# One matmul of 512 moving columns, high and low parts of h side by side, in place of two of 256 with the same weights

## The chip, the cores and the metric

The kernel runs on 1 core of one Trainium2 chip. The time is the device time of one execution in microseconds (us), taken as the median of the runs shown. TensorE multiplies: a block of 128x128 weights is loaded (the stationary operand) and the moving columns stream past it into PSUM, a memory of eight banks, each with 512 fp32 values per partition. VectorE (DVE) and ScalarE (ACT) read PSUM and work in SBUF, GpSimd (POOL) does a few large passes, SyncE (SP) issues nearly all DMAs.

## The reference

One decoder layer, batch 1, 256 tokens (S), 2048 channels (D), fp32:

```
h = LN(x)
p = h @ w_in                 # 3 groups: RG-LRU, block-sparse attention (NSA), attention into mem
h = LN(alpha*h + concat(lru, nsa, mem) @ w_out)
h = LN(alpha*h + (gelu(g) * u) @ w_down)     # g, u = causal conv3(h @ w_up)
```

`w_in` has 3608 columns, `w_up` 11264 (two times 5632), `w_out` and `w_down` 2048. The results are wanted in fp32.

## The kernel before

All large products run in fp32r, a format in which TensorE takes a 128-row by N-column moving operand in one pass but keeps fewer bits than fp32. To get the bits back each operand is split into a high part (its value rounded to fp32r) and a low part (what is left). A product a·b is then formed as aH·bH + aL·bH + aH·bL, three matmuls into one PSUM group.

**The weight stream.** The weights come as a list of chunks (`steps`) of 128 x 1024 fp32, 512 KB each. `advance` keeps four raw loads in flight (SP), has ACT write the high part (`wH`, line 127) and DVE the low part (`wL`, line 135) two to three chunks before the products use them. `run` takes chunk by chunk: `advance`, the chunk's products (`mm`), what follows them (`after`), and a round of background work (`pump`). Each engine works through its instructions in the order in which the code wrote them, and starts one when those it depends on are done; nothing else orders the work.

**Stages, in order.** Keys and values of mem (lines 272 and 205 to 208), the input norm that fills the tiles of h, the input projection in blocks of 128 channels, with the attention heads and the LRU as background work, the output projection (0.31 to 0.40 ms of the trace), the first norm, the up projection (0.41 to 0.90 ms), the down projection and the last norm.

**Channel-major blocks.** The input projection's 28 blocks and the up projection's 88 are computed by `t_mm`: one block of 128 channels is two chunks of eight 128x128 weight blocks. Per weight block of `wH` there is a matmul with the high part of h (`hH`, line 194) and one with the low part (`hL`, line 195), both of 256 moving columns (the tokens); then eight matmuls of `wL` with `hH` (line 197). So a chunk is 24 matmuls, a block 48, and the sum stands in 256 columns of a bank (`acc`, three banks, or `sc`, two). h lies in eight tiles `h0` to `h7` of four channel blocks each, the first four for high parts, the last four for low parts.

**Reading the bank.** For the up projection, `after` lets ACT write scale times bank plus bias (line 870), two DVE operations add the shifted taps from the bank (line 873), ACT applies gelu to the first half of a pair (line 876), DVE multiplies the second half in (line 878), and ACT and DVE split the product into `actH` and `actL` (lines 187, 188). In the input projection ACT or DVE copies the bank out (lines 375, 397, 429, 497), or ACT and DVE form a convolution from it (387, 390), or DVE adds an embedding to it (421).

**Token-major blocks.** Output and down projection (`proj`, `m_mm`, lines 205 to 208) use the activations as weights and the chunk as moving operand, 512 columns a matmul. In their last column block some chunks are held in other tiles (`alt`): in the down projection in `h0` to `h7`, where h is no longer needed.

Of the kernel before, what the change touches and what calls it, by code (L numbers as in the profile page):

```python
# [41 lines left out]
# column offsets in the per-partition parameter array  # L42
# [9 lines left out]
NP1 = _P["convw"].start          # up to here: parameters kept for the whole kernel  # L52
# [3 lines left out]
def hymba_layer(ctx, tc, x, memT, params, rows, wab, w1, wmem, win, wvg, wout, wup, wdn, out):  # L56
# [13 lines left out]
    hq = [fix.tile([128, 4, S], F32R, name="h%d" % i) for i in range(8)]  # L70

    def hH(kt, cols=slice(0, S)):
        return hq[kt // 4][:, kt % 4, cols]

    def hL(kt, cols=slice(0, S)):
        return hq[4 + kt // 4][:, kt % 4, cols]
# [11 lines left out]
    # ---------------------------------------------------------------- weight stream  # L88
# [26 lines left out]
    def part_tile(j, k, name, bufs):  # L115
        if steps[j]["alt"]:
            pool, names = steps[j]["alt"]
            return pool().tile([128, NE], F32R, name=names[k])
        return ws.tile([128, NE], F32R, name=name, bufs=bufs)
# [23 lines left out]
    def advance():  # L143
        """the loads run ahead of the high parts, those one chunk ahead of the low parts, those LOOK chunks ahead
        of the products"""
# [10 lines left out]
    def pump(rounds):  # L156
        """one stage of every live chain a round; at most one chain starts in a round"""
# [27 lines left out]
    # ---------------------------------------------------------------- helpers  # L185
# [4 lines left out]
    def t_mm(acc, h, l, kts, first, last):  # L190
        n = len(kts)
        for a, kt in enumerate(kts):
            w = h[:, a * 128:(a + 1) * 128]
            T.matmul(acc, w, hH(kt), start=(first and a == 0), stop=False, skip_group_check=True)  # L194
            T.matmul(acc, w, hL(kt), start=False, stop=False, skip_group_check=True)  # L195
        for a, kt in enumerate(kts):
            T.matmul(acc, l[:, a * 128:(a + 1) * 128], hH(kt), start=False,  # L197
                     stop=(last and a == n - 1), skip_group_check=True)

# [21 lines left out]
    # ---------------------------------------------------------------- first loads  # L221
# [23 lines left out]
    # loads that follow those of a chunk of the weight stream  # L245
# [6 lines left out]
    # ---------------------------------------------------------------- memory keys and values  # L252
# [46 lines left out]
    # ---------------------------------------------------------------- input norm  # L299
# [19 lines left out]
    def to_hT(tp, kt0, nk, cols, g, b, eng):  # L319
        """tp: psum [128, nk, n], channels on partitions; gain and bias, then both parts into the tiles of h"""  # L320
# [9 lines left out]
        split_act(hq[kt0 // 4][:, k:k + nk, cols], hq[4 + kt0 // 4][:, k:k + nk, cols], tv)  # L330

    def transposed(m, kt0, nk, tag):
        """normed rows of half m, channel blocks kt0.., channels on partitions"""
# [20 lines left out]
    # ---------------------------------------------------------------- input projection, channel-major blocks  # L354
    def win_blocks(cols, done, interleave=False):
        cur = {}

        def half(a, col, hf):
            def mm(h, l):
                if hf == 0:  # L360
                    cur[a] = pp.tile([128, S], F32, name="acc", bufs=3)
# [9 lines left out]
    # memory queries  # L371
    def done_qmem(a, bank):
        if a == 0:
            qms[0] = mx.tile([128, 4, S], F32, name="qmem")
        A.activation(qms[0][:, a, :], bank, AF.Copy)
        bg.append(mem_attention(a))

    # LRU input: causal convolution straight from PSUM
    xc = {}

    def done_lrux(a, bank):
# [3 lines left out]
        src = bank  # L385
        cw = lambda k: P("convw", a * 4 + k)
        A.activation(t, src, AF.Identity, scale=cw(3), bias=P("convb", a))
# [6 lines left out]
    def done_q(a, bank):  # L394
        if a == 0:
            qns[0] = mx.tile([128, 4, S], F32, name="qn")
        A.activation(qns[0][:, a, :], bank, AF.Copy)
# [13 lines left out]
    def done_cmp(a, bank):  # L411
        """stack token parities on partitions and add the position embedding"""
        src = bank.rearrange("p (n l two) -> p n l two", l=8, two=2)
# [14 lines left out]
    def done_kk(a, bank):  # L428
        A.activation(kk[:, a, :], bank, AF.Copy)
# [27 lines left out]
    # block compression  # L457
# [33 lines left out]
    # LRU output gate  # L491
    ygs = {}

    def done_lruy(a, bank):
        if a % 4 == 0:
            ygs[a // 4] = mx.tile([128, 4, S], F32, name=("qmem", "kmem")[a // 4])
        V.tensor_copy(ygs[a // 4][:, a % 4, :], bank)
# [568 lines left out]
```

## Time and profile before

| | |
|---|---|
| median of 3 runs | 1156.81 us (1154.85 to 1161.25) |
| profiled execution, span from first to last instruction | 1158.0 us |
| PE busy | 1125.6 us, 97% |
| DVE busy | 739.9 us, 64% |
| ACT busy | 568.3 us, 49% |
| matmuls, lines 194, 195 and 197 | 1856 each (1152 into `acc`, 704 into `sc`) |

The profile is one execution. Matmuls overlap in it, so that a busy PE says only that it never stood still. What one matmul costs in a row of them is the distance from start to start: the length of a stretch divided by the number of matmuls that started in it. A row of the view by stretches counts also the one or two that were still running when the stretch began.

### The profile page before, as it was taken

The page shows a single profiled execution, that of the slowest core. Times are in us where ns is not written, and L with a number is a line of the kernel's source. Part 1 is how long each engine was busy: PE and PEld are TensorE (multiplying, and loading weights), DVE is VectorE, ACT ScalarE, POOL GpSimd, SP SyncE. Part 2 cuts the span into 40 slices and gives each one's busy share as a digit, 9 for nine tenths or more (in the row PEclk, how much of TensorE's full clock was granted, in tenths as well). Part 3 has the DMA queues.
Part 4 walks back from the last instruction along what each step waited for, and adds up shares of the span by engine and source line. Part 5 has one row for each costly group of instructions (what it writes and reads, how often), then busy time and mean ns, then how long its engine had stood idle before and what let it go on. Part 6 is the DMA issues. An engine that isn't in the chain of part 4 may idle for free.

```text
span 1158.0 us, 19330 instructions
## 1 busy us (share of the span) xinstructions
PE 1125.6 (97%) x7848; PEld 1033.7 (89%) x7848; DVE 739.9 (64%) x1063; ACT 568.3 (49%) x832; POOL 44.7 (4%) x39
## 2 busy tenths in 40 slices
PE   8979999999999899999999999999999999999995
PEld 7879877899988799999999999999999888888884
DVE  6895555566765776666666666666666845454556
ACT  5635445456743465555555545555555433434340
POOL 0360000000000010000000000000000000000002
PEclk9989999999999999999999999999999999999998
DMA  9646432244566565555656556565565776666661
GB/s 340 235 171 194 148 109 90 91 141 134 182 200 191 172 209 191 184 186 181 202 186 193 185 180 200 179 204 182 183 190 178 231 244 193 191 192 193 190 195 77
DMA packets 58984, 211.81 MB, mean 183 GB/s; under 512 B 6544, under 2 KB 6672, under 8 KB 58768
## 3 DMA queue, kind: packets, MB, share of 16 engines
q1 hardware_dynamic: 57024, 203.25, 54.8%
q0 software_dynamic: 1872, 7.34, 1.9%
q8 instruction: 61, 1.00, 0.4%
q14 instruction: 27, 0.22, 0.1%
HBM read 208.47 MB, written 2.10 MB: 182 GB/s over the span
## 4 chain that ended last, share of the span: by engine, by line
PE 91%; DVE 5%; issue 2%; ACT 1%; DMA 0%; POOL 0%; DVEq 0%; SPq 0%; ACTq 0%; POOLq 0%
PE acc L194 11%; PE acc L197 11%; PE acc L195 11%; PE sc L195 7%; PE sc L197 7%; PE sc L194 7%; PE acc L205 5%; PE acc L206 5%; PE acc L208 5%; PE sc L205 5%; PE sc L206 5%; PE sc L208 5%; DVE wL L135 1%; PE sc L671 1%; PE o L700 1%
## 5 line engine op out<-in xcount | busy, mean ns | idle before, releaser
L135 DVE TENSOR_TENSOR wL<-raw,wH 128x1024 fp32r<-128x1024 f32 (+2 forms) x367 | 450.4, 1239 | 172.5 <-PE sc L208 120.8
L127 ACT ACTIVATE wH<-raw 128x1024 fp32r<-128x1024 f32 (+2 forms) x367 | 375.4, 1046 | 199.1 <-PE sc L206 159.3
L194 PE MATMUL acc<-h,wH 128*128 128x256 f32 x1152 | 283.3, 285 | 4.8 <-ACT h L187 4.8
L195 PE MATMUL acc<-h,wH 128*128 128x256 f32 x1152 | 278.2, 281 | 2.6 <-DVE h L188 2.6
L194 PEld LDWEIGHTS acc<-h,wH 128*128 128x128 f32 x1152 | 218.4, 190 | 5.6 <-ACT h L187 5.2
L195 PEld LDWEIGHTS acc<-h,wH 128*128 128x128 f32 x1152 | 219.0, 190 | 3.3 <-DVE h L188 3.0
L194 PE MATMUL sc<-h,wH 128*128 128x256 f32 x704 | 168.5, 280 | 0.0
L195 PE MATMUL sc<-h,wH 128*128 128x256 f32 x704 | 168.3, 279 | 0.0
L197 PE MATMUL acc<-h,wL 128*128 128x256 f32 x1152 | 160.7, 281 | 0.0
L197 PEld LDWEIGHTS acc<-h,wL 128*128 128x128 f32 x1152 | 147.1, 190 | 0.0
L195 PEld LDWEIGHTS sc<-h,wH 128*128 128x128 f32 x704 | 132.7, 188 | 0.0
L194 PEld LDWEIGHTS sc<-h,wH 128*128 128x128 f32 x704 | 131.9, 187 | 0.0
L197 PE MATMUL sc<-h,wL 128*128 128x256 f32 x704 | 97.4, 279 | 0.0
L873 DVE SCALAR_TENSOR_TENSOR tn<-sc,prm,tn 128x255 f32<-128x255 f32 x88 | 42.4, 482 | 82.9 <-ACT tn L870 81.4
L197 PEld LDWEIGHTS sc<-h,wL 128*128 128x128 f32 x704 | 89.0, 188 | 0.0
L873 DVE SCALAR_TENSOR_TENSOR tn<-acc,prm,tn 128x255 f32<-128x255 f32 x88 | 42.4, 482 | 44.3 <-ACT tn L870 42.7
L205 PE MATMUL sc<-wH,actH 128*128 128x512 f32 x168 | 66.0, 393 | 0.0
L205 PE MATMUL acc<-wH,actH 128*128 128x512 f32 x168 | 66.0, 393 | 0.0
L206 PE MATMUL acc<-wH,actL 128*128 128x512 f32 x168 | 65.7, 391 | 0.0
L206 PE MATMUL sc<-wH,actL 128*128 128x512 f32 x168 | 65.7, 391 | 0.0
L870 ACT ACTIVATE tn<-sc,prm 128x256 f32<-128x256 f32 x44 | 24.8, 563 | 65.4 <-PE sc L197 65.4
L208 PE MATMUL sc<-wL,actH 128*128 128x512 f32 x168 | 51.9, 390 | 0.0
(300 smaller groups left out, 1241.6 us busy)
## 6 DMA issues: line engine op xcount, KB each, us to landing
raw<-in_wup_dram SPq DMA_DIRECT2D x176, 512.0 KB, 4.3
raw<-in_wdn_dram SPq DMA_DIRECT2D x88, 512.0 KB, 4.2
raw<-in_win_dram SPq DMA_DIRECT2D x56, 512.0 KB, 3.3
raw<-in_wout_dram SPq DMA_DIRECT2D x32, 512.0 KB, 4.0
raw<-in_wmem_dram SPq DMA_DIRECT2D x15, 512.0 KB, 6.5
raw<-in_wvg_dram SPq DMA_DIRECT2D x5, 420.0 KB, 4.1
res<-in_x_dram SPq DMA_DIRECT2D x4, 512.0 KB, 7.3
g<-in_rows_dram POOLq DMA_DIRECT2D x4, 512.0 KB, 6.6
```

Of the source, the lines that this page charges most:

```text
L127: A.activation(h[:, s], raws[j][:, s], AF.Copy)
L135: V.tensor_sub(l[:, s], r[:, s], splits[j][0][:, s].bitcast(F32))
L194: T.matmul(acc, w, hH(kt), start=(first and a == 0), stop=False, skip_group_check=True)
L195: T.matmul(acc, w, hL(kt), start=False, stop=False, skip_group_check=True)
L197: T.matmul(acc, l[:, a * 128:(a + 1) * 128], hH(kt), start=False, stop=(last and a == n - 1), skip_group_check=True)
L205: T.matmul(acc, xh(kt, ms), h[:, w], start=(first and a == 0), stop=False)
L206: T.matmul(acc, xl(kt, ms), h[:, w], start=False, stop=False)
L208: T.matmul(acc, xh(kt, ms), l[:, a * N:(a + 1) * N], start=False, stop=(last and a == n - 1))
L671: T.matmul(s[:, :, :nk], qn[rows_, j, qs], kk[rows_, :, :nk], start=True, stop=False, skip_group_check=True)
L700: T.matmul(outs[q][rows_, j, :], vv[:, k, b * 128 + g * 64:b * 128 + g * 64 + 64], pT[:, b * (q + 1) + k, :], start=False, stop=(b == 1 an ...
L870: A.activation(t, src, AF.Identity, scale=P("fcw", cb * 3 + 2), bias=P("fcb", cb))
L873: V.scalar_tensor_tensor(t[:, s:], src[:, :S - s], P("fcw", cb * 3 + k), t[:, s:], op0=OP.mult, op1=OP.add)
```

## The change

High and low part of four channel blocks of h lie now in one tile, `h0` to `h3` of [128, 2, 4, 256], at the addresses that the eight tiles had. `hB(kt)` is the moving operand of 512 columns: 256 of the high part and, 4 KB further on, 256 of the low part. `t_mm` issues one matmul per high weight block, into both halves of a bank, and the low weight blocks add to the first half. When a block is done, `total` has ACT copy the second half to SBUF and DVE add the first half to the copy. What read the bank reads the sum in SBUF: a tile `y` with one buffer, or the destination itself. The scaling of the convolutions moves from ACT to DVE. Tiles for the held chunks are taken in pairs.

```diff
-    hq = [fix.tile([128, 4, S], F32R, name="h%d" % i) for i in range(8)]
+    hq = [fix.tile([128, 2, 4, S], F32R, name="h%d" % i) for i in range(4)]
...
+    def hB(kt):
+        return hq[kt // 4][:, :, kt % 4, :]
...
         for a, kt in enumerate(kts):
-            w = h[:, a * 128:(a + 1) * 128]
-            T.matmul(acc, w, hH(kt), start=(first and a == 0), stop=False, skip_group_check=True)
-            T.matmul(acc, w, hL(kt), start=False, stop=False, skip_group_check=True)
+            T.matmul(acc, h[:, a * 128:(a + 1) * 128], hB(kt), start=(first and a == 0), stop=False,
+                     skip_group_check=True)
         for a, kt in enumerate(kts):
-            T.matmul(acc, l[:, a * 128:(a + 1) * 128], hH(kt), start=False,
+            T.matmul(acc[:, 0, :], l[:, a * 128:(a + 1) * 128], hH(kt), start=False,
                      stop=(last and a == n - 1), skip_group_check=True)
+
+    def total(dst, bank):
+        A.activation(dst, bank[:, 1, :], AF.Copy)
+        V.tensor_add(dst, dst, bank[:, 0, :])
...
-        A.activation(qms[0][:, a, :], bank, AF.Copy)
+        total(qms[0][:, a, :], bank)
...
-        src = bank
+        src = sm.tile([128, S], F32, name="y", bufs=1)
+        total(src, bank)
         cw = lambda k: P("convw", a * 4 + k)
-        A.activation(t, src, AF.Identity, scale=cw(3), bias=P("convb", a))
+        V.tensor_scalar(t, src, cw(3), P("convb", a), op0=OP.mult, op1=OP.add)
...
-        A.activation(qns[0][:, a, :], bank, AF.Copy)
+        total(qns[0][:, a, :], bank)
...
-        src = bank.rearrange("p (n l two) -> p n l two", l=8, two=2)
+        y = sm.tile([128, S], F32, name="y", bufs=1)
+        total(y, bank)
+        src = y.rearrange("p (n l two) -> p n l two", l=8, two=2)
...
-        V.tensor_copy(ygs[a // 4][:, a % 4, :], bank)
+        total(ygs[a // 4][:, a % 4, :], bank)
...
-                    cur[u] = pp.tile([128, S], F32, name=("acc", "sc")[u], bufs=(3, 2)[u])
+                    cur[u] = pp.tile([128, 2, S], F32, name=("acc", "sc")[u], bufs=(3, 2)[u])
...
-                src = cur[u]
+                src = sm.tile([128, S], F32, name="y", bufs=1)
+                total(src, cur[u])
                 cb = u * FB + i
-                A.activation(t, src, AF.Identity, scale=P("fcw", cb * 3 + 2), bias=P("fcb", cb))
+                V.tensor_scalar(t, src, P("fcw", cb * 3 + 2), P("fcb", cb), op0=OP.mult, op1=OP.add)
...
-         (lambda: fix, ["h%d" % i for i in range(8)]), lambda a: None)
+         (lambda: fix, [("h%d" % i,) for i in range(4)]), lambda a: None)
```

On TensorE a chunk of the up projection (the second one of a block into `sc`) stood like this before; `h_76` and `h_77` are two tiles of high parts, `h_80` and `h_81` those of the low parts of the same channels:

```order
L194 MATMUL sc<-h_76,wH 128x256
L195 MATMUL sc<-h_80,wH 128x256
L194 MATMUL sc<-h_76,wH 128x256
L195 MATMUL sc<-h_80,wH 128x256
L194 MATMUL sc<-h_76,wH 128x256
L195 MATMUL sc<-h_80,wH 128x256
L194 MATMUL sc<-h_76,wH 128x256
L195 MATMUL sc<-h_80,wH 128x256
L194 MATMUL sc<-h_77,wH 128x256
L195 MATMUL sc<-h_81,wH 128x256
L194 MATMUL sc<-h_77,wH 128x256
L195 MATMUL sc<-h_81,wH 128x256
```

The same chunk, and the one after it, with the change, where `h_74` to `h_77` hold both parts and line 200 is the wide matmul, 203 that of the low weights:

```order
L200 MATMUL sc<-h_76,wH 128x512 x4
L200 MATMUL sc<-h_77,wH 128x512 x4
L203 MATMUL sc<-h_76,wL 128x256 x4
L203 MATMUL sc<-h_77,wL 128x256 x4
L200 MATMUL acc<-h_74,wH 128x512 x4
L200 MATMUL acc<-h_75,wH 128x512 x4
L203 MATMUL acc<-h_74,wL 128x256 x4
L203 MATMUL acc<-h_75,wL 128x256 x4
```

Sixteen matmuls of 256 columns became eight of 512; the eight with the low weights stay.

On DVE a pair of blocks of the up projection stood like this before, first half from `acc`, second from `sc`:

```order
L873 SCALAR_TENSOR_TENSOR tn<-acc,prm,tn 128x255
L873 SCALAR_TENSOR_TENSOR tn<-acc,prm,tn 128x254
L135 TENSOR_TENSOR wL<-raw,wH 128x1024 x2
L873 SCALAR_TENSOR_TENSOR tn<-sc,prm,tn 128x255
L873 SCALAR_TENSOR_TENSOR tn<-sc,prm,tn 128x254
L878 TENSOR_TENSOR tn<-tn 128x256
L188 TENSOR_TENSOR actL<-tn,actH 128x256
L135 TENSOR_TENSOR wL<-raw,wH 128x1024 x2
```

With the change line 209 is the addition in `total`, 886 the scaling, 889, 894, 195 and 142 are the former 873, 878, 188 and 135:

```order
L209 TENSOR_TENSOR y<-y,acc 128x256
L886 TENSOR_SCALAR tn<-y,prm 128x256
L889 SCALAR_TENSOR_TENSOR tn<-y,prm,tn 128x255
L889 SCALAR_TENSOR_TENSOR tn<-y,prm,tn 128x254
L142 TENSOR_TENSOR wL<-raw,wH 128x1024 x2
L209 TENSOR_TENSOR y<-y,sc 128x256
L886 TENSOR_SCALAR tn<-y,prm 128x256
L889 SCALAR_TENSOR_TENSOR tn<-y,prm,tn 128x255
L889 SCALAR_TENSOR_TENSOR tn<-y,prm,tn 128x254
L894 TENSOR_TENSOR tn<-tn 128x256
L195 TENSOR_TENSOR actL<-tn,actH 128x256
L142 TENSOR_TENSOR wL<-raw,wH 128x1024 x2
```

Two operations come in ahead of each block's taps, and the low parts of the weights queue behind them as they queued behind the taps before.

## Rows read from the trace of the kernel before

**Rows 1.** The page: busy time of the engines.

```profile
PE 1125.6 (97%) x7848; PEld 1033.7 (89%) x7848; DVE 739.9 (64%) x1063; ACT 568.3 (49%) x832; POOL 44.7 (4%) x39
```

**Rows 2.** The page: chain that ended last, by engine.

```profile
PE 91%; DVE 5%; issue 2%; ACT 1%; DMA 0%; POOL 0%; DVEq 0%; SPq 0%; ACTq 0%; POOLq 0%
```

**Rows 3.** Busy time by stretches (length, engines with counts, clock, DMA share, GB/s).

```profile
450.00:850.00 400.00, 400.00 (x3431) 400.00 (x3430) 264.40 (x359) 206.44 (x286) 0.00 (x0) 1.00 0.59 189
320.00:385.00 65.00, 65.00 (x280) 52.40 (x279) 41.13 (x46) 27.72 (x30) 0.00 (x0) 1.00 0.63 190
910.00:1120.00 210.00, 210.00 (x919) 172.31 (x918) 109.34 (x97) 81.36 (x77) 2.10 (x4) 1.00 0.66 203
...
1139.04:1144.18 5.14, 5.14 (x23) 4.13 (x22) 5.07 (x9) 0.82 (x1) 3.25 (x3) 1.00 0.13 51
390.62:392.89 2.27, 2.27 (x11) 1.88 (x10) 2.20 (x2) 2.03 (x2) 0.00 (x0) 1.00 0.91 244
```

**Rows 4.** Timeline of PE in the down projection's end (start us, length us).

```profile
1139.28 0.39 PE L205 MATMUL sc<-h,actH 128*128 128x512 f32 x1
```

**Rows 5.** Timeline of PE: two moving runs of 128 columns, then 512 together.

```profile
116.98 0.70 PE L671 MATMUL sc<-kk,qn 64*128 64x256 f32 x2 [0.47 <-ACT qn L397]
117.61 0.28 PE L672 MATMUL sc<-diagb,identb 128*128 128x256 bf16 x1
...
161.93 1.12 PE L671 MATMUL sc<-kk,qn 64*128 64x512 f32 x2
162.99 0.28 PE L672 MATMUL sc<-diagb,identb 128*128 128x256 bf16 x1
```

**Rows 6.** Chain in order of time (start us, us): fp32, 256 columns in one run.

```profile
261.11 1.73 PE sc L601 x8
```

**Rows 7.** Groups of instructions with shapes apart (busy us, mean ns, idle before).

```profile
L135 DVE TENSOR_TENSOR wL<-raw,wH 128x1024 fp32r<-128x1024 f32 x359 | 443.5, 1247 | 170.8 <-PE sc L208 120.8 <-ACT wH L127 26.0 <-PE acc L197 15.3
...
L194 PE MATMUL acc<-h,wH 128*128 128x256 f32 x1152 | 283.3, 285 | 4.8 <-ACT h L187 4.8
L195 PE MATMUL acc<-h,wH 128*128 128x256 f32 x1152 | 278.2, 281 | 2.6 <-DVE h L188 2.6
...
L870 ACT ACTIVATE tn<-acc,prm 128x256 f32<-128x256 f32 x44 | 24.8, 563 | 51.8 <-PE acc L197 51.8
...
L873 DVE SCALAR_TENSOR_TENSOR tn<-acc,prm,tn 128x255 f32<-128x255 f32 x44 | 21.3, 483 | 42.7 <-ACT tn L870 42.7
...
L878 DVE TENSOR_TENSOR tn<-tn 128x256 f32<-128x256 f32 x44 | 18.7, 426 | 1.5
...
L685 DVE TENSOR_SCALAR P<-P,sw 128x256 f32<-128x256 f32 x16 | 4.9, 351 | 0.3
...
L397 ACT ACTIVATE qn<-acc 128x256 f32<-128x256 f32 x4 | 1.5, 384 | 8.4 <-PE acc L197 8.4
```

**Rows 8.** Timeline of DVE, one pair of the up projection.

```profile
612.05 1.00 DVE L873 SCALAR_TENSOR_TENSOR tn<-sc,prm,tn 128x255 f32<-128x255 f32 x2 [1.88 <-ACT tn L870]
...
614.00 0.42 DVE L188 TENSOR_TENSOR actL<-tn,actH 128x256 fp32r<-128x256 f32 x1 [0.48 <-ACT actH L187]
614.34 2.35 DVE L135 TENSOR_TENSOR wL<-raw,wH 128x1024 fp32r<-128x1024 f32 x2
617.65 1.00 DVE L873 SCALAR_TENSOR_TENSOR tn<-acc,prm,tn 128x255 f32<-128x255 f32 x2 [0.96 <-ACT tn L870]
...
620.15 1.23 DVE L135 TENSOR_TENSOR wL<-raw,wH 128x1024 fp32r<-128x1024 f32 x1 [0.37 <-ACT wH L127]
```

**Rows 9.** Timeline and chain around the block compression and the first head.

```profile
78.58 2.46 DVE L421 TENSOR_TENSOR P<-acc,prm 64x120 f32<-64x120 f32 x8
...
81.67 1.98 PE tp L467 x32
...
116.54 0.38 ACT L397 ACTIVATE qn<-acc 128x256 f32<-128x256 f32 x1 [1.69 <-PE acc L197]
```

**Rows 10.** Line 671: what PE waited for before it (us, times).

```profile
  ACT qn L397: 2.3, 4
```

More of the change, by code (lines that the diff above doesn't have):

```diff
@@ L69, in hymba_layer @@
     prm2 = mx.tile([128, NP - NP1], F32, name="prm2")
-    hq = [fix.tile([128, 4, S], F32R, name="h%d" % i) for i in range(8)]
+    hq = [fix.tile([128, 2, 4, S], F32R, name="h%d" % i) for i in range(4)]
     def hH(kt, cols=slice(0, S)):
-        return hq[kt // 4][:, kt % 4, cols]
+        return hq[kt // 4][:, 0, kt % 4, cols]
     def hL(kt, cols=slice(0, S)):
-        return hq[4 + kt // 4][:, kt % 4, cols]
+        return hq[kt // 4][:, 1, kt % 4, cols]
+    def hB(kt):
+        return hq[kt // 4][:, :, kt % 4, :]
     res = fix.tile([128, 2, D], F32, name="res")
@@ L117, in part_tile @@
             pool, names = steps[j]["alt"]
-            return pool().tile([128, NE], F32R, name=names[k])
+            if len(names) == 2:
+                return pool().tile([128, NE], F32R, name=names[k])
+            if k == 0:
+                steps[j]["both"] = pool().tile([128, 2, NE], F32R, name=names[0])
+            return steps[j]["both"][:, k, :]
         return ws.tile([128, NE], F32R, name=name, bufs=bufs)
@@ L329, in to_hT @@
         k = kt0 % 4
-        split_act(hq[kt0 // 4][:, k:k + nk, cols], hq[4 + kt0 // 4][:, k:k + nk, cols], tv)
+        split_act(hq[kt0 // 4][:, 0, k:k + nk, cols], hq[kt0 // 4][:, 1, k:k + nk, cols], tv)
     def transposed(m, kt0, nk, tag):
@@ L360, in mm @@
                 if hf == 0:
-                    cur[a] = pp.tile([128, S], F32, name="acc", bufs=3)
+                    cur[a] = pp.tile([128, 2, S], F32, name="acc", bufs=3)
                 t_mm(cur[a], h, l, list(range(hf * 8, hf * 8 + 8)), hf == 0, hf == 1)
@@ L428, in done_kk @@
     def done_kk(a, bank):
-        A.activation(kk[:, a, :], bank, AF.Copy)
+        total(kk[:, a, :], bank)
     vv = mx.tile([128, 2, 256], F32, name="vv")
@@ L738, in proj @@
                 k = c - (nk2 - HOLD + 1)
+                held = nb == 3 and 0 <= k
                 chunk(src[nb, kord[2 * c] // 2], NE, mm,
                       (lambda nb=nb, accs=accs: both(nb, accs[1])) if c == nk2 - 1 else None,
-                      alt=(alt[0], alt[1][2 * k:2 * k + 2]) if nb == 3 and k >= 0 else None)
+                      alt=(alt[0], alt[1][k]) if held else None)
     def ln1_first(nb, acc):
@@ L764, in hpart @@
     def hpart(off, m, kt0, nk):
-        return hq[off + kt0 // 4][:, kt0 % 4:kt0 % 4 + nk, m * 128:(m + 1) * 128]
+        return hq[kt0 // 4][:, off, kt0 % 4:kt0 % 4 + nk, m * 128:(m + 1) * 128]
     def hi(m, kt0, nk):
@@ L770, in lo @@
     def lo(m, kt0, nk):
-        V.tensor_sub(hpart(4, m, kt0, nk), tns.pop((m, kt0)), hpart(0, m, kt0, nk).bitcast(F32))
+        V.tensor_sub(hpart(1, m, kt0, nk), tns.pop((m, kt0)), hpart(0, m, kt0, nk).bitcast(F32))
     def ln1_between(a):
@@ L838, in hymba_layer @@
     proj(8, KORD, wout, aH, aL, ln1_first, ln1_both,
-         (lambda: mx, ("lruR", "lruI", "lruT", "qmem", "kmem", "vmem", "qn", "xc0")), ln1_between)
+         (lambda: mx, (("lruR", "lruI"), ("lruT", "qmem"), ("kmem", "vmem"), ("qn", "xc0"))), ln1_between)
     n_out = len(steps)
```

## The prediction

> **What bounds the kernel now.** I read the page's busy times first: PE is busy for 97% of the span, DVE for 64% and ACT for 49% [rows 1]. The chain that ended last lies on PE for 91% [rows 2]. So only three things can move the time: what a row of matmuls costs from start to start, what makes PE stand still, and what happens after its last matmul. The change leaves the last one alone.
>
> Next the view by stretches, to get that distance. From 450 to 850 us only the up projection runs: 3431 matmuls of 256 columns counted, two of them still running from before, so 400 / 3429 = 0.1167 us each; DVE is busy 264 us of the 400 and ACT 206, the granted clock is 1.00, its upper level (2.4 GHz), as in all stretches below, and PE never waits [rows 3]. The output projection (320 to 385) runs matmuls of 512 columns: 65 / 279 = 0.2330 us each. That is exactly twice the matmul of half its width. The down projection (910 to 1120) runs 512 columns at 210 / 918 = 0.2288 [rows 3].
>
> **The main term: one matmul of 512 for two of 256.** 1856 pairs (1152 + 704) become 1856 single matmuls. A pair costs 2 x 0.1167 = 0.2333 us now. What the wide one will cost, no row shows for these operands, since its moving operand is a tile of h in two pieces and its weights come from the weight stream. The rows around it:
>
> - 0.2330, output projection, moving operand from the weight stream.
> - 0.2288, down projection, moving operand also from the weight stream, other weights.
> - From 1139.04 to 1144.18 the moving operand is one of the tiles of h, 512 columns [rows 4]: 22 started, 5.14 / 22 = 0.2336.
> - 0.227, from 390.62 to 392.89, moving operand in tiles further up in SBUF: 10 started in 2.27 us. It is the lowest distance in any stretch of 512 columns [rows 3].
>
> The ends are therefore 0.227 and 0.2336 for one piece. I take 0.2333, no change: whenever h streams, with 256 columns in the up projection or with 512 at the end, it costs 0.456 ns a column. A fixed price per instruction would have to show as a lower cost per column at 512, and in the two rows nearest to the new matmul it doesn't. The row is limited per column, by the rate at which the operand comes in, and the number of columns stays. The weight loads that go (1856 of them) gave nothing away either: PE's loads are busy 400 us of 400 at 256 columns and 52 of 65 at 512, at the same cost per column [rows 3].
>
> Does the gap between the two pieces cost? Line 671 has a moving operand of two runs of 128 columns, and later one run of 512. From the first of its two matmuls to the matmul of line 672 behind them it is 117.61 - 116.98 = 0.63 us, and with 512 columns 162.99 - 161.93 = 1.06 [rows 5]. So 256 more columns take 0.215 us a matmul, and 256 columns in one run take 1.73 / 8 = 0.216 at line 601 [rows 6]: had the break between the runs a price, the difference would be smaller than that by it. These are fp32 rows, which stream slower; for fp32r the break may still show. I take 0 and leave up to 5 ns per matmul, 9 us, for a rival.
>
> Main term: 0 us, bounds -1856 x 6.3 ns = -11.7 us and about +9 us.
>
> **What the change adds behind each block.** Per block of the up projection ACT's 0.563 us from the bank becomes a copy of 0.384 (as line 397's), and DVE gets an addition from the bank, between 0.426 (line 878, from SBUF) and 0.483 (line 873, from PSUM), I take 0.43, and a scaling of 0.351 (line 685) [rows 7]. Per pair of blocks that is 1.56 us more on DVE. A pair takes PE 96 x 0.1167 = 11.2 us, and DVE is busy 264.4 / 400 x 11.2 = 7.4 of it; after, about 9.0. The cover is there, but the order on DVE counts: I follow one pair [rows 8]. The taps start at 612.05 today, behind ACT's 0.56; with copy, addition and scaling, and 0.03 of handing on for each, they start near 612.7. Everything behind them moves by 0.66: the product, the split, and two low parts (2.35) until about 617.3. The next block ends on PE at 617.06 (the taps' 617.65 less 0.59), its copy is there at 617.47, so DVE isn't late; addition and taps last until 619.3, the two low parts, with the wait of 0.37 for their high part behind a gelu that is 0.66 later, until about 622.0. The next copy arrives at 623.05. So some 1.0 us in 11.2 stays free, and the low parts are made more than a chunk (2.8 us) ahead of use. PE should see nothing: 0 us. ACT gains 0.18 us a block.
>
> **Where PE does stand still for such work.** Three places, all in the input projection or at the first block of the up projection:
>
> - The first heads need `qn` from the bank at once. PE waited 2.3 us in total, four times, for ACT's copy [rows 10]. Now DVE's addition comes behind the copy, 0.43 + 0.05 each time. Two matmuls, each with its weight load, make up the four: +1.0 us (0 to 2).
> - The block compression: the eight additions on DVE end at 78.58 + 2.46 = 81.04 and PE starts to use them at 81.67 [rows 9]: 0.63 in hand, against 0.384 + 0.43 + 0.05 = 0.86 that come before them. +0.25 us.
> - Where PE waits for new tiles of h (4.8 us for high and 2.6 for low parts in all [rows 7]), the matmul with the high part used to run before the low part had come. Now the wide one starts after both: 0.12 us later, at some four places. +0.5 us.
>
> The LRU and attention stages get 28 additions and 8 scalings more on DVE, about 15 us beside PE work of 250 us. DVE's waits there are for PE; I put +0.3 us for what shows. The additions need a second pass over `acc` banks, but a bank comes free earlier, since the taps read SBUF. Tiles taken in pairs at the end of the two projections wait for the same last readers as before: 0.
>
> **Sum.** 0 + 1.0 + 0.25 + 0.5 + 0.3 = +2 us on the profiled execution: 1158.0 becomes 1160. The profile shows no other time than its span, and that is 1.2 us above the median of the runs, inside their spread. So on the median: 1156.8 + 2 = **1158.8 us**.
>
> **Rivals.**
>
> *The instruction has a fixed price, and a pair then pays it once.* For it: the two stretches below 0.2333. At the down projection's 0.2288 a pair saves 4.5 ns, 8.3 us in all; at 0.227 it saves 6.3 ns, 11.7 us. With the +2 from above: 1150.5 or 1147.1. Against it: neither of those stretches has h as moving operand, and the one that has stands at 0.2336. The Trainium skill ("TensorE: Matmul & The Clock Gate", Back-to-back issue gap) says that the isolated distance at the full clock is N / 2.4 + 2.5 ns and that in a stream of loads and matmuls both set the spacing. By that figure the pair would fall by 2.5 ns, an estimate of 4.6 us, and the kernel would come out near 1154. The rows don't agree with its size: 0.1167 stands here against 0.1092, and 0.2330 against 0.2158.
>
> *DVE becomes the bound of the up projection.* The place is the first addition after a pair's second block. It decides once DVE needs more than 11.2 us per pair, that is, if addition, scaling and handing on come to 1.0 us per pair more than I put (0.25 per operation): then the low parts fall behind pair by pair, the lead of a chunk is used up, and PE waits. At 0.2 to 0.4 us beyond that, 44 pairs lose 9 to 18 us: 1168 to 1177. For it: only a tenth of the pair is left free, and the chain from bank to split gets longer. Against: the durations are measured here.
>
> *The two pieces of the moving operand cost something at each matmul.* At 5 ns it is +9 us, 1168; below 2 ns it can't be told. Line 671 speaks against it.
>
> **How the numbers follow.** The forecast 0.54, the fixed price 0.30, DVE 0.10, the two pieces 0.06. About 0.5%, 5.8 us, is what a measurement of this kernel can tell from no change. The forecast's own range is 1156 to 1162, all but 0.01 of it within 0.5%. Of the fixed price 0.24 is faster (8.3 or 11.7 less 2) and 0.06, at the smaller price, is not. Of DVE 0.09 is slower, of the two pieces 0.04. Faster 0.24, within 0.62, slower 0.14. The range goes from 1147 (the fixed price in full) to 1166 (leaving out most of the two slow cases).
>
> **What would show it.** Right: in the up projection's middle, 16 matmuls per chunk in 2.80 us, the wide ones 0.233 apart, the narrow ones 0.1167; DVE busy near 80% of that stretch and PE without a wait; PE's waits before line 671's successor up by about 1 us. Wrong: chunks of 2.76 us or less (the fixed price), waits of PE for `wL` there (DVE), or chunks above 2.82 with no wait at all (the two pieces).

## The result and the profile after

The changed kernel takes 1166.37 us, the median of 4 runs (1165.21 to 1168.25); the kernel before took 1156.03 beside it (1154.85 to 1161.25). The ratio is 1.0087, 95% interval 1.0072 to 1.0103: slower by 10 us. The forecast was 1158.8, the range 1147 to 1166, and "slower by over 0.5%" had a chance of 0.14. In the batches below, with 17 to 29 executions of the kernel before in each, that kernel stands at 1161 us, and the change made again there (e1) is 6.4 us slower. So the loss is 6 to 10 us.

The page of the changed kernel, busy times and the chain by engine, to be read against [rows 1] and [rows 2]:

```profile
PE 1126.2 (97%) x5992; PEld 948.1 (81%) x5992; DVE 819.7 (70%) x1267; ACT 553.6 (48%) x842; POOL 45.9 (4%) x39
...
PE 88%; DVE 5%; issue 2%; ACT 2%; DMA 2%; POOL 0%; DVEq 0%; SPq 0%; ACTq 0%; POOLq 0%
```

1856 matmuls and weight loads are gone, and PE is busy as long as before. The up projection's stretch of the changed kernel (columns as in [rows 3]):

```profile
450.00:850.00 400.00, 400.00 (x2287) 347.45 (x2287) 324.72 (x503) 192.19 (x286) 0.00 (x0) 1.00 0.58 188
```

In the up projection PE never waits, and 16 matmuls, 8 wide and 8 narrow, take 400 / 2287 x 16 = 2.80 us, as 24 narrow ones did before. The timeline of PE there:

```profile
600.10 1.09 PE L203 MATMUL acc<-h,wL 128*128 128x256 f32 x8
601.03 2.03 PE L200 MATMUL sc<-h,wH 128*128 128x512 f32 x8
602.90 1.09 PE L203 MATMUL sc<-h,wL 128*128 128x256 f32 x8
603.83 2.03 PE L200 MATMUL sc<-h,wH 128*128 128x512 f32 x8
```

Eight wide matmuls start within 602.90 - 601.03 = 1.87 us, 0.234 each; eight narrow ones within 0.93, 0.116 each. So the up projection neither gains nor loses, and the loss lies ahead of it: a block near its start begins at 421.9 us instead of 415.3, and from there to the last matmul the distance between the two profiled executions stays at 6.6 us. (The run's time is the span plus 1.9 us: 1164.3 and 1166.19 here. So before's profiled execution, span 1158.0, was itself some 4 us above its median, and the full 10 us don't show between these two traces.)

Where PE stands still in the changed kernel, with the VectorE and GpSimd instructions that matter (timeline; start us, us, in brackets what ended the idle time ahead):

```profile
70.55 3.40 DVE L142 TENSOR_TENSOR wL<-raw,wH 128x1024 fp32r<-128x1024 f32 x1
74.91 0.42 DVE L209 TENSOR_TENSOR y<-y,acc 128x256 f32<-128x256 f32 x1 [0.97 <-ACT y L208]
75.36 5.42 DVE L435 TENSOR_TENSOR P<-y,prm 64x120 f32<-64x120 f32 x8
80.81 1.23 DVE L142 TENSOR_TENSOR wL<-raw,wH 128x1024 fp32r<-128x1024 f32 x1
82.41 2.80 DVE L435 TENSOR_TENSOR P<-y,prm 64x120 f32<-64x120 f32 x8
...
72.82 3.37 POOL L325 TENSOR_TENSOR res<-res,xc 128x1024 f32<-128x1024 f32 x1
76.27 2.48 POOL L327 TENSOR_TENSOR res<-res,lruR 128x1024 f32<-128x1024 f32 x1
...
80.63 2.70 PE L481 MATMUL tp<-P,raw 128*64 128x30 f32 x32 [3.09 <-DVE P L435]
...
119.54 0.70 PE L685 MATMUL sc<-kk,qn 64*128 64x256 f32 x2 [0.93 <-DVE qn L209]
...
294.72 1.13 PE L615 MATMUL sc<-xc,wab 128*128 128x256 f32 x4 [2.24 <-ACT lruI L618]
...
306.14 0.42 DVE L209 TENSOR_TENSOR kmem<-kmem,acc 128x256 f32<-128x256 f32 x1 [2.51 <-ACT kmem L208]
...
313.87 0.42 DVE L209 TENSOR_TENSOR kmem<-kmem,acc 128x256 f32<-128x256 f32 x1 [1.21 <-ACT kmem L208]
...
318.61 0.73 PE L219 MATMUL acc<-wL,oH 128*128 128x512 f32 x2 [1.34 <-DVE wL L142]
```

Read it in two places. The eight additions of the first block compression took 2.46 us before [rows 9], where GpSimd had finished 1.1 us ahead of them. The same eight now take 5.42 us, the first 3.4 of them beside GpSimd's gain and bias, and eight more a few microseconds later, when GpSimd is done, take 2.80; the low part of a weight chunk likewise takes 3.40 beside GpSimd and 1.23 alone. In the LRU stage VectorE stands idle for 2.51 and 1.21 us at the addition of the two halves, until ScalarE's copy arrives; low parts of weights are queued behind that addition, and at 318.61 PE waits for one.

### The profile page after: what moved, and what is told of

It is laid out like the page before. It is cut to its first block, busy times and chain, and to the rows that moved or that the text cites. A ratio compares the mean times of both kernels' runs of the same rounds, so it can differ in the third digit from the quotient of the medians.

```text
span 1164.3 us, 15806 instructions
## 1 busy us (share of the span) xinstructions
PE 1126.2 (97%) x5992; PEld 948.1 (81%) x5992; DVE 819.7 (70%) x1267; ACT 553.6 (48%) x842; POOL 45.9 (4%) x39
## 4 chain that ended last, share of the span: by engine, by line
PE 88%; DVE 5%; issue 2%; ACT 2%; DMA 2%; POOL 0%; DVEq 0%; SPq 0%; ACTq 0%; POOLq 0%
PE acc L200 21%; PE sc L200 14%; PE acc L203 11%; PE sc L203 7%; PE acc L219 5%; PE acc L216 5%; PE acc L217 5%; PE sc L219 5%; PE sc L216 5%; PE sc L217 4%; PE sc L685 1%; PE o L714 1%; DMA raw<-in_wmem_dram 1%; DVE wL L142 1%; DMA raw<-in_win_dram 1%
## 5 line engine op out<-in xcount | busy, mean ns | idle before, releaser
L200 PE MATMUL acc<-h,wH 128*128 128x512 f32 x1152 | 301.1, 402 | 6.2 <-DVE h L195 6.2
L200 PEld LDWEIGHTS acc<-h,wH 128*128 128x128 f32 x1152 | 208.5, 190 | 47.0 <-DVE h L195 7.2
L200 PE MATMUL sc<-h,wH 128*128 128x512 f32 x704 | 179.3, 395 | 0.0
L200 PEld LDWEIGHTS sc<-h,wH 128*128 128x128 f32 x704 | 125.3, 188 | 23.6
L889 DVE SCALAR_TENSOR_TENSOR tn<-y,prm,tn 128x255 f32<-128x255 f32 (+1 forms) x176 | 85.1, 484 | 6.3
L194 ACT ACTIVATE actH<-tn 128x256 fp32r<-128x256 f32 x44 | 18.4, 418 | 107.2 <-DVE tn L894 104.7
L219 PE MATMUL acc<-wL,actH 128*128 128x512 f32 x168 | 52.3, 393 | 0.0
L209 DVE TENSOR_TENSOR y<-y,sc 128x256 f32<-128x256 f32 x44 | 18.6, 422 | 43.8 <-ACT y L208 43.7
L208 ACT ACTIVATE y<-acc 128x256 f32<-128x256 f32 x54 | 20.8, 384 | 39.4 <-PE acc L203 34.4
L886 DVE TENSOR_SCALAR tn<-y,prm 128x256 f32<-128x256 f32 x88 | 36.3, 412 | 3.2
```

The costliest lines, as they stand in the source:

```text
L194: A.activation(dh, src, AF.Copy)
L200: T.matmul(acc, h[:, a * 128:(a + 1) * 128], hB(kt), start=(first and a == 0), stop=False, skip_group_check=True)
L208: A.activation(dst, bank[:, 1, :], AF.Copy)
L209: V.tensor_add(dst, dst, bank[:, 0, :])
L219: T.matmul(acc, xh(kt, ms), l[:, a * N:(a + 1) * N], start=False, stop=(last and a == n - 1))
L886: V.tensor_scalar(t, src, P("fcw", cb * 3 + 2), P("fcb", cb), op0=OP.mult, op1=OP.add)
```

## The experiments

All kernels of a batch ran on one chip beside the kernel before, whose median there was 1161.49, 1160.68, 1161.11, 1160.91 and 1161.02 us in the order of the batches. Where kernels of different batches are compared, it is by their ratios to it. In these kernels a list names the blocks that take the wide form, the others keep three narrow matmuls per weight block and one read of the bank; line numbers therefore differ from the changed kernel's.

**Which kind of block loses: the first batch.** The edit is the list:

```
e1: WIDE = ("cmp", "kk", "q", "qm", "lrux", "lruy", "up")   (the change)
e2: WIDE = ("up",)
e3: e1 without "cmp"
e4: e3 without "kk", "q", "qm"
```

> The change as it is, again, to time it on the chip of the runs it is compared with. Both theories: ratio 1.007 to 1.010 to the kernel before. Theory A (the time is lost where TensorE waits in the input projection for what reads the banks) expects the up projection's chunks at 2.80 us as before, and every loss before 320 us of the trace. Theory B (the wide form itself costs, by two-piece operands or by a VectorE that can't follow in the up projection) would need chunks above 2.80 us or waits there.

> The wide matmul in the up projection alone (88 of 116 blocks, 1408 of 1856 pairs); the input projection as before. Theory A: ratio 1.000 (0.998 to 1.002), since nothing waits in the up projection. Theory B: three quarters of the loss stay, ratio 1.0065. The prediction's rival of a fixed price per matmul: ratio 0.993.

> Wide everywhere except in the two blocks of the block compression, which read the bank as before. Theory A with the compression as its largest part (its additions read SBUF twice while GpSimd is at work: 5.4 us in place of 2.5, TensorE waits 3.1 us, and its clock falls for 3.4 us more): 3 to 5 us faster than the full change, ratio 1.005 or so. If the compression is only the 0.25 us of the prediction: ratio 1.0085, as the full change.

> As the run before, and the blocks of kk, q and the memory queries (10 blocks) are as before too; wide are the LRU blocks and the up projection. Theory A: another 1 to 2 us less (two waits of the first heads, 0.5 us each, and some in the memory attention), ratio 1.003; what is left is the LRU stage's. If the loss is all the compression's: no difference to the run before.

Measured: e1 1167.88 us, ratio 1.0058 (1.0038 to 1.0077); e3 1161.53, 1.0011 (0.9995 to 1.0026); e4 1159.48, 0.9988 (0.9974 to 1.0001); e2 1156.48, 0.9949 (0.9931 to 0.9966). Taken one from the other: block compression costs 6.4 us, queries and keys 2.0, the LRU blocks 3.0. What is left, the up projection with 1408 of the 1856 wide matmuls, stands 5 us below the kernel before, and neither theory had that. All four ratios lie below what was expected. The kernel before was slower in this batch than beside the result (1161.49 against 1156.03), which would account for it; the differences between the four don't hang on it.

**What the layout does by itself.** e5 keeps the joint tiles of h, with an empty list.

> Only the layout of the change: high and low parts of h in joint tiles, but every product as before (512 columns nowhere, three matmuls of 256 per weight block, PSUM read once). Theory L (the joint tiles or their dependences are worth something by themselves, and explain that the kernel with the wide form in the up projection alone was 5 us faster than before): 0.993 to 0.997 of before, about 1156. Rival U (the wide form in the up projection brings the 5 us): 1.000 of before. Rival S (before wanders by itself on its first 90 us, by which stretches fall to the lower TensorE clock): anywhere between, and a layout-only trace whose first 90 us hold one half-clock stretch of 6.8 us where before holds two.

1160.17 us, 0.9991 (0.9974 to 1.0009): by this median the layout is worth nothing, and theory L fails. Rival U isn't proved by that, though the two ratios differ by 5 us: e2 and e5 have the same profiled span, 1155.1 us, with the same waits. e5's runs spread from 1156.9 to 1165.7, e2's from 1154.5 to 1158.2; why is not settled. e8 and e12, below, compare the two forms again.

e5 and e1 have equal layouts, so their timelines show where the wide form loses. Starts of the same PE instruction:

| PE instruction | e5 | e1 | behind by |
|---|---|---|---|
| chunk ahead of the compression, `acc<-h,wL` | 73.51 | 73.91 | 0.40 |
| transposes of the first block, `tp<-P,raw` | 78.53 | 81.99 | 3.46 |
| next chunk, `acc<-h,wL` | 82.48 | 87.45 | 4.97 |
| second head, `sc<-kk,qn` | 121.95 | 127.63 | 5.68 |
| memory attention, `o<-PT,vmem` | 246.00 | 252.37 | 6.37 |
| chunk after the LRU gates, `acc<-h,wH` | 287.35 | 295.27 | 7.92 |
| next chunk, `acc<-h,wL` | 289.41 | 298.79 | 9.38 |
| output projection, `acc<-wL,oH` | 308.95 | 319.94 | 10.99 |

The spans differ by 10.8. The jump of 1.51 at the compression and that of 1.46 behind the gates are no waits. The stretches of e1:

```profile
82.00:88.00 6.00, 6.00 (x45) 5.25 (x46) 5.78 (x13) 2.22 (x3) 0.00 (x0) 0.72 0.48 175
294.00:300.00 6.00, 5.51 (x21) 4.67 (x22) 2.01 (x2) 3.85 (x8) 0.00 (x0) 0.72 0.80 237
```

and the first of them in e5:

```profile
82.00:88.00 6.00, 6.00 (x54) 6.00 (x53) 4.24 (x8) 1.56 (x3) 0.00 (x0) 1.00 0.81 272
```

A mean of 0.72 over 6 us is 3.4 us at the lower level (1.2 GHz, half) in each of the two, and PE had stood still just before: 2.7 us for the compression, 2.2 at the gates. So in e1 each of these waits costs itself and about 1.5 us more. That is not the same in every execution. The changed kernel's own profile has these two rows, after waits of 3.1 us at the compression and 2.2 at the gates:

```profile
82.00:88.00 6.00, 6.00 (x27) 5.16 (x27) 5.41 (x12) 1.26 (x2) 0.00 (x0) 0.50 0.60 188
294.00:300.00 6.00, 5.28 (x27) 4.63 (x28) 3.14 (x4) 5.39 (x12) 0.00 (x0) 1.00 0.75 223
```

The clock is low for the whole 6 us behind the compression and not at all behind the gates. After gate waits of 2.2 to 2.4 us it fell in e1, e6 and e10 and stayed at 1.00 in the changed kernel, e3, e4, e7 and e18; what decides it is not shown.

**Why the compression loses.** e6 runs the residual's gain and bias on VectorE; e7 leaves them on GpSimd, but later:

```
e6  -    bg.append(gain_bias(G))
    +    bg.append(gain_bias(V))
e7  +    for b in range(2):
    +        G.tensor_copy(hold, blkt[b][:, 15, 1, 14:15])
         bg.append(gain_bias(G))
```

> The change, but the eight 128x1024 multiplications and additions of gain and bias on the residual run on VectorE, queued behind the additions of block compression, where they ran on GpSimd at 55 to 79 us. Theory C (the loss of block compression is VectorE, now with two SBUF inputs, slowed beside GpSimd's work): the first additions P<-y take 2.8 us instead of 5.4, the low parts of weights 1.23 instead of 3.4, PE's wait of 3.1 us before the transposes at 77 us falls under 1, and the time falls by about 6 us, to 1.000 to 1.002 of before. Rival W (the added copy and addition of the two halves are themselves the chain that PE waits for): additions faster, but the wait stays at 2 us or more and the time within 2 us of the change, 1.006 or more of before; VectorE's extra 9 us may then even add to it.

> The change, with GpSimd's gain and bias held back by two 1-column copies that read the finished blocks of compression, so that the same GpSimd work runs from about 84 us on instead of beside the compression. Theory C: additions at 2.8 us, PE's wait before the transposes under 1 us, some 4 to 6 us less than the change, unless the low parts of weights that then run beside GpSimd (3.4 us instead of 1.23, two per 5.6 us of chunk) starve PE at 84 to 106 us, which would give back 1 to 3 of it. Rival W: as the change, 1.006 or more of before.

e6: 1164.82 us, 1.0032 (1.0020 to 1.0044). Its timeline:

```profile
71.85 2.84 DVE L460 TENSOR_TENSOR P<-y,prm 64x120 f32<-64x120 f32 x8
...
74.53 2.05 PE L506 MATMUL tp<-P,raw 128*64 128x30 f32 x32 [0.65 <-DVE P L460]
...
115.12 1.22 PE L710 MATMUL sc<-kk,qn 64*128 64x256 f32 x2 [5.68 <-DVE qn L227]
```

Theory C holds at the compression: additions 2.84, PE's wait 0.65. But only some 3 us were won, since the last five steps of gain and bias were run in one piece, and the first head waits 5.68 us for `qn` behind them, with a mean granted clock of 0.59 from 114 to 120 us. The 3 us alone would not show theory C, since the same move helps the kernel with narrow products about as much (e5 to e8, below).

e7: 1167.42, 1.0056 (1.0035 to 1.0077), no gain. Its timeline:

```profile
71.76 2.85 DVE L461 TENSOR_TENSOR P<-y,prm 64x120 f32<-64x120 f32 x8
...
85.55 1.58 DVE L607 TENSOR_SCALAR lc<-prm 128x8 f32<-128x8 f32 x1
87.16 2.29 DVE L608 TENSOR_TENSOR lc<-lc,prm 128x8 f32<-128x8 f32 x1
...
92.06 3.00 DVE L144 TENSOR_TENSOR wL<-raw,wH 128x840 fp32r<-128x840 f32 x1
...
87.06 2.37 POOL L344 TENSOR_TENSOR res<-res,xc 128x1024 f32<-128x1024 f32 x1
89.51 2.37 POOL L346 TENSOR_TENSOR res<-res,lruR 128x1024 f32<-128x1024 f32 x1
...
95.12 1.07 PE L238 MATMUL acc<-wL,h 128*128 128x280 f32 x3 [3.78 <-DVE wL L144]
...
103.91 1.07 PE L238 MATMUL acc<-wL,h 128*128 128x280 f32 x3 [2.88 <-DVE wL L144]
```

The additions are as quick as in e6, and the loss came back elsewhere: now other VectorE work lies beside GpSimd. Eight elements a partition, 0.17 us alone, take 1.6 to 2.3, and PE waits 3.78 and 2.88 us for low parts. That is more than the 1 to 3 us allowed for, and the granted clock is at its lower level, 0.50, from 96 to 102 us besides. So theory C was right in kind and the give-back too small. e7 differs from the change in one more thing: its tile `hold` moves tiles made after it, and the up projection runs at the matmul prices of the kernels with moved tiles below (2293 matmuls in the 400 us, e18 2292, the change 2287).

e10 leaves GpSimd where it was and takes one SBUF operand away from every addition:

```
-            total(y, bank, "cmp")
+            y = bank[:, 0, :]
...
+                        V.tensor_tensor(b, b, low[g * 64:g * 64 + 64, hb:hb + 15, :, par], op=OP.add)
```

> The change, but block compression adds straight from the bank: eight additions of the position rows to the first half, eight more that add the second half in place; each of the 32 reads one operand in PSUM and one in SBUF, and the copy and the addition of the halves ahead of them go. GpSimd's gain and bias run at the same time as in the change. Theory C (two SBUF inputs beside GpSimd's work): sixteen additions take twice 2.5 us, 4.9 to 5.2 us a block, the first block included, against 0.8 + 5.4 and 0.8 + 2.8 in the change; PE's wait of 3.1 us at 77 us falls to 1 to 2.5 us, since the first block is earlier and the second later. Rival (any VectorE instruction is slowed beside GpSimd): the sixteen of the first block take 8 to 11 us, and the wait grows by 2 us or more.

1165.18 us, 1.0038 (1.0024 to 1.0051). Its timeline:

```profile
74.35 2.59 DVE L459 TENSOR_TENSOR P<-acc,prm 64x120 f32<-64x120 f32 x8 [0.55 <-PE acc L213]
76.97 2.69 DVE L470 TENSOR_TENSOR P<-P,acc 64x120 f32<-64x120 f32 x8
...
72.68 3.38 POOL L343 TENSOR_TENSOR res<-res,xc 128x1024 f32<-128x1024 f32 x1
76.13 2.37 POOL L345 TENSOR_TENSOR res<-res,lruR 128x1024 f32<-128x1024 f32 x1
```

PE's wait at the compression is 2.32 us, inside the 1 to 2.5 expected. Twice eight additions take 5.28 us in the same place where eight took 5.42: beside GpSimd an addition with one operand in PSUM keeps its pace (2.59 for eight), one with both in SBUF does not. Without GpSimd's work the sixteen take the same, 2.59 and 2.65 in e13 below. e5 shows it too, with the additions as they were before the change and GpSimd at work all the time:

```profile
75.46 2.52 DVE L460 TENSOR_TENSOR P<-acc,prm 64x120 f32<-64x120 f32 x8 [0.34 <-PE acc L206]
...
74.00 3.37 POOL L343 TENSOR_TENSOR res<-res,xc 128x1024 f32<-128x1024 f32 x1
77.45 2.37 POOL L345 TENSOR_TENSOR res<-res,lruR 128x1024 f32<-128x1024 f32 x1
```

The Trainium skill has this ("SBUF — State Buffer", Who interferes with whom): a VectorE instruction with two SBUF inputs contends with a GpSimd instruction that reads SBUF, and one with at most one SBUF input, outside the two-port modes, does not. The traces agree and give the size here: 5.42 against 2.80.

**Why the LRU loses.** e9 reads both halves of the LRU gate blocks on VectorE:

```
-        A.activation(dst, bank[:, 1, :], AF.Copy)
+        if kind == "lruy":
+            V.tensor_copy(dst, bank[:, 1, :])
+        else:
+            A.activation(dst, bank[:, 1, :], AF.Copy)
         V.tensor_add(dst, dst, bank[:, 0, :])
```

> The change, but where the eight LRU gate blocks are read out of the bank, both halves are read by VectorE (a copy, then the addition in place), with no copy on ScalarE in between. Theory Q (VectorE, which works in order, stands behind the addition until ScalarE's copy comes, 2.52 and 1.21 us at 299 and 307 us, and the low parts of weights queued behind it come late): PE's wait of 1.50 us for wL at 317 us goes, that of 2.49 us at 292 us falls by 0 to 0.8; 1.5 to 2.3 us less than the change, 1.004 to 1.0045 of before where the change had 1.0058 and 1.0087. Rival R (VectorE simply has too much to do there, some 0.4 us more per block either way): no wait gets shorter, the time is the same as the change's or up to 1 us longer.

1164.71 us, 1.0034 (1.0020 to 1.0048). Its timeline:

```profile
293.15 1.13 PE L643 MATMUL sc<-xc,wab 128*128 128x256 f32 x4 [1.63 <-ACT lruI L646]
...
304.03 0.42 DVE L230 TENSOR_TENSOR kmem<-kmem,acc 128x256 f32<-128x256 f32 x1
...
315.73 0.73 PE L240 MATMUL acc<-wL,oH 128*128 128x512 f32 x2
```

VectorE does more work and nobody waits: the addition follows its copy at once, PE's wait for `wL` is gone, that at the gates is 1.63 instead of 2.24, and no stretch of lower clock follows it. Theory Q holds; the gain, 2.8 us against e1 by the ratios, is a little above its upper end. e1's stretch of lower clock at the gates may be the difference, but the changed kernel's profile has none there, so that is not shown.

**Is that the whole loss?** e13 makes three repairs: gain and bias on VectorE ahead of the LRU constants (one step per chunk), e9's edit, e10's edit. e16 takes e10's back.

> The change with all three repairs at once: gain and bias on VectorE, one step per chunk and queued ahead of the LRU constants, so that none is left to be run in one piece; block additions straight from the bank; LRU gate blocks read out by VectorE alone. If the waits named so far are the whole loss, what is left of it is 0.9 us at the first two scores, 0.7 us of memory attention and 0.9 us at the LRU's gates: 2 to 3.5 us above the up-wide kernel of this batch, 0.995 to 0.998 of before. Rival (something else in the wide form of the input projection costs time, in the products themselves or in the clock): 1.000 of before or more.

> The change with two repairs: gain and bias on VectorE ahead of the LRU constants, and LRU gate blocks read out by VectorE alone; block compression with copy and addition again. Of the run with three repairs, where sixteen additions a block took 5.1 us and PE waited 2.45 us for them, PE's wait falls to about 0.7 and one stretch of lower clock behind it may go: 1.7 to 3.5 us less, 0.997 to 0.9985 of before. The wait of 2.8 us at the first head, where the addition for qn stands behind what VectorE still has queued, stays. Rival (more than these waits is wrong with the wide form in the input projection): 1.000 of before.

e13: 1160.84 us, 1.0003 (0.9992 to 1.0014); e16: 1160.33, 0.9990 (0.9974 to 1.0006). Both miss the times expected: e13 lands where its rival stood, e16 between expectation and rival. The wait for the compression is 2.29 us in e13, where sixteen additions are simply longer, and in e16 it is small:

```profile
75.51 1.70 PE L509 MATMUL tp<-P,raw 128*64 128x30 f32 x26 [0.38 <-DVE P L463]
...
113.06 0.70 PE L713 MATMUL sc<-kk,qn 64*128 64x256 f32 x2 [2.65 <-DVE qn L230]
```

The other wait stayed: `qn` used to need ScalarE alone, and its addition now stands in VectorE's queue. With 1.5 us for each of two stretches of lower clock that e14, below, doesn't have, and 0.9 us more at the gates, about 7 of the 8 us between e16 and e14 are named (in the traces e16 is 8.9 us behind at the first norm). The rest is not shown.

**The narrow kernel without GpSimd's work, and the best version.** e8 has an empty list and gain and bias on VectorE; e12 the up projection wide besides; e14 also puts gain and bias ahead of the LRU constants.

> Layout only (all products narrow) with gain and bias on VectorE. If GpSimd's work beside VectorE costs the narrow kernel too (low parts of weights at 3.4 us, stretches of lower clock at 62 to 69 us): 2 to 4 us faster than layout only, about 0.991 of before if theory L holds. Rival: it was hidden, and 9 us more of VectorE cost 0 to 2 us.

> The wide form in the up projection alone, gain and bias on VectorE. Theory N (the wide form is worth nothing and costs nothing where VectorE and ScalarE have room): same as layout only with gain on VectorE, 0.992 to 0.996 of before. Rival U (the wide form gives some 4 us in the up projection): 0.990.

> The wide form in the up projection alone, gain and bias on VectorE ahead of the LRU constants, one step per chunk. PE's wait of 1.1 us for wL at 112 us, where five steps had been run in one piece, goes: 0.992 of before. Rival: the steps delay low parts of weights one by one, and it stays at 0.993 or above.

e8: 1153.18 us, 0.9939 (0.9917 to 0.9961); e12: 1153.06, 0.9931 (0.9912 to 0.9950); e14: 1151.59, 0.9923 (0.9906 to 0.9941). e14 beats both kernels. The wide form has no part in that as far as e8 and e12 show, which agree within their intervals, as theory N had it; a narrow e14 was not run. GpSimd's work beside VectorE costs the kernel with narrow products too: 6 us by the ratios of e5 and e8, but 3.7 by their profiled spans (1155.1 and 1151.4) and 2 by the ratios of e2 and e12.

**Is the wide matmul worth nothing in itself?** In e11, e15, e17 and e18 the weight stream's tiles start 32 bytes further on in each partition; these two lines are all that differs from e8, e14, e5 and e1. Other tiles made after `pad` can move with them, but of the operands of the up projection's matmuls only the weights do, since the tiles of h are made before it:

```
+    pad = fix.tile([128, 8], F32, name="pad")
+    V.memset(pad, 0.0)
```

> Layout only with gain and bias on VectorE, and 32 bytes per partition left free ahead of the weight stream's tiles, so that these start on multiples of 256 bytes as the tiles of h do; nothing else differs. Theory P (the matmul's 116.7 ns per 256 columns depends on how the two operands' addresses lie to each other, as other pairs of tiles in this trace take 113.3 to 114.4): 113.3 ns per 256 columns in the up projection, 14 us less, 0.982 of before. Rival: 116.7 as before, 0.994.

> As the kernel before this one, with the 32 bytes left free ahead of the weight stream's tiles that made the 256-column matmul 120.0 ns instead of 116.7. Theory S (the price depends on the place of both operands and on how many columns go through per weight block): the 512-column matmul takes 230 ns there, as the few 512-column products with such addresses do in the earlier traces (115 per 256), the 256-column one 120; in all within 2 us of the kernel before this one. Rival: 240 ns, and 17 us more, as in the narrow kernel.

> Layout only, all products narrow, nothing repaired, with the 32 bytes ahead of the weight stream's tiles. 5568 matmuls of 256 columns at 120.0 instead of 116.7 ns: 18 us more than layout only without the shift, 1.014 to 1.017 of before.

> The change, nothing repaired, with the same 32 bytes. Theory S (what one wide matmul is worth against two narrow ones depends on how the two operands lie): 1856 wide ones at 230.8, 1856 narrow ones at 119.1, so the time stays at the change's, 1.005 to 1.009 of before, and some 7 to 10 us below the narrow kernel with the same shift: with the operands so placed the same change makes the kernel faster. Rival: 240 and 120, 1.02 to 1.025 of before, and the change still costs 8 to 10 us.

e11: 1170.42 us, 1.0078 (1.0059 to 1.0097), 16 us slower than e8. Theory P has it backwards: the up projection's stretch in e11 is

```profile
450.00:850.00 400.00, 400.00 (x3335) 400.00 (x3335) 257.34 (x348) 201.34 (x278) 0.00 (x0) 1.00 0.56 183
```

that is 0.1200 us a matmul. e15, wide in the same place, takes 1154.66 us, 0.9949 (0.9932 to 0.9966), 3 us above e14, where 2 were allowed: its input projection is narrow and pays 0.1200 too. Without any repair e17, narrow, takes 1176.47 us, 1.0139 (1.0110 to 1.0169), and e18, wide, 1165.44, 1.0045 (1.0031 to 1.0058). The timeline of PE in e18:

```profile
600.29 2.00 PE L212 MATMUL sc<-h,wH 128*128 128x512 f32 x8
602.13 1.11 PE L215 MATMUL sc<-h,wL 128*128 128x256 f32 x8
603.08 2.00 PE L212 MATMUL sc<-h,wH 128*128 128x512 f32 x8
```

0.230 us per wide matmul, against 2 x 0.120 for the pair it replaces. With the tiles 32 bytes further on, the same change makes the kernel 11 us faster (1176.47 to 1165.44), although it still has the waits found above. Theory S holds, with both times a little below the ranges given. No time is won over the unmoved tiles by that: e18 stays above e5 (1160.17). The pair of narrow matmuls went from 0.233 to 0.240 us, the wide one from 0.234 to 0.230.

## Why the forecast was wrong, step by step

- *Main term 0.* Right here: 0.234 us measured, 0.2333 taken. The reason given, that the price goes by the column, held only for the addresses at hand, so there was luck in the term. With the weights 32 bytes further the same 512 columns take 0.240 or 0.230 by form. The rivals of a fixed price and of two costly pieces didn't occur at these addresses.
- *Up projection 0.* Right: VectorE busy 324.72 of 400 us, 81% where "near 80%" was forecast, PE without a wait. Addition 0.422, copy 0.384, scaling 0.412 instead of 0.351.
- *qn +1.0.* Right: two waits of PE, 0.47 us each before [rows 5], are 0.93 each after, 0.92 more.
- *New tiles of h +0.5.* Right in size: 0.40 behind at 73.9 us.
- *Block compression +0.25.* Wrong, and the largest single miss: 3.1 us behind and 1.5 more by the lower clock after it, e1 against e5. The step added 0.86 us ahead of the eight additions and kept their 2.46 us [rows 9]. But with the new copy in SBUF these additions read two SBUF operands where one had been `acc`, in PSUM, and GpSimd was running beside them. The rows to see it in were there, in the timeline of VectorE before: the same low part takes 3.40 us while GpSimd works (until 77.5 us) and 1.23 after it. By the times of that one trace GpSimd was done when the additions began at 78.58; in e5 they begin at 75.46, while it works, so the rows gave the cost and only a second execution would have given the overlap.

```profile
75.17 3.40 DVE L135 TENSOR_TENSOR wL<-raw,wH 128x1024 fp32r<-128x1024 f32 x1
...
81.07 1.23 DVE L135 TENSOR_TENSOR wL<-raw,wH 128x1024 fp32r<-128x1024 f32 x1
```

- *LRU and attention +0.3.* Wrong: 0.7 at memory attention, 1.5 at the gates with 1.5 of lower clock behind, 1.6 at the output projection's first low part, 5.3 in all, e1 against e5; the lower clock at the gates is missing from the changed kernel's own profile. The step compared sums of busy time (15 us beside 250). It didn't ask what is queued behind an addition that waits for another engine.
- *Lower clock.* No term at all; in e1 the two more stretches cost the 3 us counted in the two points above.
- *From the span to the median.* "The profile shows no other time than its span" was wrong by 1.9 us a run; the sum was a difference, so nothing hung on it.

So the step that failed is "Where PE does stand still for such work", by its terms for compression and LRU: 0.55 us forecast, about 10 measured between e5 and e1. In its place the runs show additions slowed by a second operand in SBUF beside GpSimd, and low parts of weights late behind additions that wait for ScalarE.

## What to carry to other kernels

When an operand moves from PSUM to SBUF, price every reader again: a VectorE instruction that now has two SBUF inputs can take longer while GpSimd works beside it (here 5.42 us for eight, against 2.52). When one read becomes a copy on one engine and an addition on another, look at what is queued behind the addition on an in-order engine, at each place where PE had less than a few tenths of a microsecond in hand. And a price per column read from one layout holds for that layout: move the tiles by 32 bytes before concluding that a matmul form is worth nothing.

## What the hardware did that was not expected

- 32 bytes in the start of the weight tiles move a matmul of 256 columns from 0.1167 to 0.1200 us and one of 512 from 0.234 to 0.230: the wide form is worth nothing at one place and some 10 ns a pair at the other.
- In the profiled execution of e16 the granted clock stood at 0.95 for nearly the whole span. The up projection ran no slower, 2288 matmuls as at 1.00 in e14; the down projection did, 902 matmuls where e14 and the kernel before have 919, 0.233 us each instead of 0.229. That makes 4 us, about as much as this execution (1164.50) lies above e16's median:

```profile
450.00:850.00 400.00, 400.00 (x2288) 347.50 (x2287) 324.54 (x502) 191.88 (x285) 0.00 (x0) 0.95 0.57 190
910.00:1120.00 210.00, 210.00 (x902) 170.10 (x901) 109.18 (x96) 79.52 (x75) 2.10 (x4) 0.95 0.59 202
```
